# Loading x from ScalarE's queue, shaping the first weight pieces, and letting softmax scalings choose among three engines

## The chip, the cores and the metric

The kernel runs on one core of a Trainium2 chip. The core has five engines that work side by side, each through its own list of instructions in order: PE (TensorE, the matmuls, with a separate track for weight loads), DVE (VectorE), ACT (ScalarE), POOL (GpSimd) and SP (SyncE, which here only issues DMAs). An instruction that waits for a semaphore holds everything behind it on its engine. The metric is the device time of one execution, in microseconds (us), lower being better.

## The reference, cut to what matters

Everything is float32, one batch, 512 positions of width 1024.

```python
# first block: one RG-LRU layer (A), then one sliding-window attention layer (B)
h = rmsnorm(x, norm_g); u = h @ w_in                      # 1024 -> 2*1536
xb, gate = split(u); xb = causal_depthwise_conv(xb, conv_w, conv_b)   # width 4
r = sigmoid(blockdiag(xb, wr) + br); i = sigmoid(blockdiag(xb, wi) + bi)
a = exp(-8 * r * softplus(-lam)); b = sqrt(1 - a*a) * (i * xb)
x = x + (scan(h_t = a_t*h_{t-1} + b_t) * silu(gate)) @ w_out
k, v = rmsnorm(x, kv_g) @ w_kv                            # 2 kv heads of 64, k normed
q, gate = rmsnorm(x, b_norm_g) @ w_in                     # 16 heads of 64, q normed
p = softmax(q k^T * scale + alibi, band of 128, with a sink in the denominator)
x = x + ((p @ v) * silu(gate)) @ w_out
# second block
z = rms_norm(x, norm_mix) @ w_in     # q_a k_a v_a q_b k_b v_b g_a g_b
y_a = windowed_gqa(...)              # 8 heads, 2 kv heads, softmax with a sink
y_b = neighborhood_attn(...)         # 8 heads, 8 x 16 neighbours, a bias table
x = x + (sig(g_a) * (y_a @ w_pa) + sig(g_b) * (y_b @ w_pb)) @ w_out
x = x + relu(rms_norm(x, norm_mlp) @ w_up)**2 @ w_down    # 1024 -> 4096 -> 1024
return rms_norm(x, norm_final)
```

Each attention takes, per head and block of 128 queries, a row of exponentials, their sum, and then the product of the row with 1 / sum. That last product is the "softmax scaling" of the title.

## The kernel before, in words

x is held transposed, as 8 tiles of 128 features by 512 positions. Every large product is made of three matmuls per tile: each operand is split into a high part and a low part (`hi`, `lo`, both in a rounded form of float32), and high times high, high times low and low times high are added up in PSUM. So each weight goes through a DMA (L426) into a raw buffer of the pool `fb`, through an engine that makes the high part (a rounding copy, in the helper A at L307, which may take ACT at L322, POOL at L331 or DVE at L326) and one that makes the low part (a subtraction, TT at L346) into the pool `rb`. The matmuls come from L396, transposes by the identity from L420. The tiles of x are split in the same way, after a multiplication by the norm's weights (ACT L322, then DVE L360). The factor 1 / rms of a position comes later, as a broadcast tile that the outputs are multiplied by.

The order of work is not the program's text. A planner, class `Sched` (L82 to L210), runs while the kernel is built. Every piece of work is a generator (a task) that yields one operation after another; an operation lists the engines that may run it, with an estimated duration for each. At each step the planner picks the task and engine whose operation would end earliest by its model, with a handicap for POOL where there is a choice (AVOID, L36 and L168). What it writes is a fixed list for each engine. The names that the change touches:

- `x_load` (L1692): loads `vec` (all the small vectors) and the 8 tiles of x, each through SP's queue, the later ones held until some weights have been asked for; `x_ready` (L682) starts the split of the tile.
- `raw_task` (L449): issues the weight loads through SP in the order of a list, no more than RAW_MAX ahead; `pieces` (L446) says in what strips a loaded weight is then split; `gemm_pair` (L550) takes the first layer's weights in segments of 4 tiles.
- WARM (L31): ten matmuls on zeros (L1707) at the start. MAXU: how many attention units (a block of queries and a group of heads) may be in flight at once; it limits the tasks of `unit_slot` (L1053).
- `PMUL` (L371, issued at L374): the softmax scaling, which only POOL may run. It is also used for a multiplication of the mask by a column of the queries' deviations (L960).

In an attention unit (`attn_unit`, about L945 to L1040) the order is: scores on PE, a mask and row maximum on DVE (L972), exponentials with their sums on ACT (L322), the reciprocal on DVE (L389), the scaling on POOL (L374), the transposes of the scaled rows on PE (L420), an eviction that splits them (ACT L322, DVE L346), and the product with v on PE. PE takes other tasks' matmuls between these as far as the planner has found any.

DMAs are tracked by eight semaphores, named DMAHW0 to DMAHW7 in the listings below, taken in turn by the loads of all queues. A load that takes a semaphore again waits until that semaphore's previous load has landed.

## Time and profile before

| | |
|---|---|
| time, median of 3 runs | 1137.61 us (1136.96 to 1138.18) |
| profiled execution: its own time | 1139.5 us |
| its span (first to last instruction) | 1137.7 us |
| PE busy | 1119.6 us, 98% of the span |
| DVE, ACT, POOL busy | 758.7, 384.1, 306.6 us (67%, 34%, 27%) |
| mean granted clock of TensorE | 0.994 of full speed |

The profiled execution is 1.9 us (0.17%) above the median; 1.8 us of its time lie outside its span. In the rows, times are us from the start of the span unless they are marked ns. "Idle before" is the time in which the engine had nothing to run, and what ended it stands behind the arrow. A row that stands for several instructions says so with x and their number.

### The profile page before, as it was taken

The page shows a single profiled execution, that of the slowest core. Times are in us where ns is not written, and L with a number is a line of the kernel's source. Part 1 is how long each engine was busy: PE and PEld are TensorE (multiplying, and loading weights), DVE is VectorE, ACT ScalarE, POOL GpSimd, SP SyncE. Part 2 cuts the span into 40 slices and gives each one's busy share as a digit, 9 for nine tenths or more (in the row PEclk, how much of TensorE's full clock was granted, in tenths as well). Part 3 has the DMA queues.
Part 4 walks back from the last instruction along what each step waited for, and adds up shares of the span by engine and source line. Part 5 has one row for each costly group of instructions (what it writes and reads, how often), then busy time and mean ns, then how long its engine had stood idle before and what let it go on. Part 6 is the DMA issues. An engine that isn't in the chain of part 4 may idle for free.

```text
span 1137.7 us, 14747 instructions
## 1 busy us (share of the span) xinstructions
PE 1119.6 (98%) x5316; PEld 931.7 (82%) x5316; DVE 758.7 (67%) x1344; ACT 384.1 (34%) x781; POOL 306.6 (27%) x404
## 2 busy tenths in 40 slices
PE   8999999999999899999999999999999999999997
PEld 6788888888888688788888888888888888888887
DVE  7999998775777886568666565876554225556332
ACT  5457761234566631156444251111111111111001
POOL 1222333135586532032322224312110003113100
PEclk9999999999999899999999999999999999999998
DMA  7333445108133330820463645523233322223001
GB/s 290 87 117 107 145 141 193 56 1 257 40 96 95 134 102 12 238 102 29 134 191 111 176 133 174 185 75 111 79 117 118 112 74 89 78 93 111 1 1 74
DMA packets 46793, 127.42 MB, mean 112 GB/s; under 512 B 6272, under 2 KB 7936, under 8 KB 46720
## 3 DMA queue, kind: packets, MB, share of 16 engines
q1 hardware_dynamic: 46720, 126.47, 35.0%
q8 instruction: 42, 0.69, 0.2%
q14 instruction: 31, 0.25, 0.1%
HBM read 106.53 MB, written 2.10 MB: 95 GB/s over the span
## 4 chain that ended last, share of the span: by engine, by line
PE 93%; DVE 2%; issue 2%; DMA 1%; ACT 1%; POOL 1%; SPq 0%; POOLq 0%; DVEq 0%
PE ps L396 90%; PE ps L420 3%; DVE fb L360 1%; DMA fb<-in_mk 1%; POOL fb L374 0%; DMA fb<-in_x 0%; DVE rb L346 0%; SPq L426 0%; ACT rb L322 0%; DVE fb L346 0%; ACT fb L322 0%; DMA rb<-rb 0%; DVE fb L972 0%; DVE fb L1632 0%; POOLq L1846 0%
## 5 line engine op out<-in xcount | busy, mean ns | idle before, releaser
L396 PE MATMUL ps<-rb 128*128 128x512 f32 (+2 forms) x4856 | 1087.1, 383 | 5.1 <-DMA rb<-rb 1.6
L396 PEld LDWEIGHTS ps<-rb 128*128 128x128 f32 x4856 | 878.0, 188 | 177.6 <-issue 3.0
L331 POOL TENSOR_SCALAR rb<-fb 128x1024 fp32r<-128x1024 f32 (+5 forms) x163 | 175.5, 1087 | 564.2 <-PE ps L396 407.4
L346 DVE TENSOR_TENSOR rb<-fb,rb 128x1024 fp32r<-128x1024 f32 (+5 forms) x305 | 289.0, 972 | 40.9 <-ACT rb L322 37.1
L322 ACT ACTIVATE rb<-fb 128x512 fp32r<-128x512 f32 (+4 forms) x131 | 96.9, 745 | 307.0 <-DVE fb L360 155.4
L346 DVE TENSOR_TENSOR fb<-ps,fb 128x512 f32<-128x512 f32 (+3 forms) x142 | 83.6, 590 | 156.7 <-PE ps L396 141.0
L374 POOL TENSOR_SCALAR fb<-fb,sm 128x256 f32<-128x256 f32 (+2 forms) x128 | 74.9, 603 | 125.3 <-DVE sm L389 97.1
L346 DVE TENSOR_TENSOR fb<-fb 128x512 f32<-128x512 f32 (+1 forms) x120 | 88.9, 747 | 23.3 <-ACT rb L322 21.1
L360 DVE SCALAR_TENSOR_TENSOR fb<-ps,fb 128x512 f32<-128x512 f32 x56 | 38.5, 688 | 58.4 <-PE ps L396 58.3
L346 DVE TENSOR_TENSOR rb<-ps,rb 128x512 fp32r<-128x512 f32 (+2 forms) x86 | 52.3, 612 | 37.5 <-ACT rb L322 35.5
L322 ACT ACTIVATE fb<-fb 128x512 f32<-128x512 f32 (+1 forms) x66 | 39.4, 612 | 102.6 <-DVE fb L346 83.7
L322 ACT ACTIVATE rb<-ps 128x512 fp32r<-128x512 f32 (+2 forms) x86 | 46.0, 538 | 82.1 <-PE ps L420 73.8
L322 ACT ACTIVATE fb<-fb,sm 128x256 f32<-128x256 f32 (+2 forms) x128 | 65.2, 512 | 21.2 <-DVE sm L368 16.1
L322 ACT ACTIVATE rb<-fb,vec 128x512 fp32r<-128x512 f32 x41 | 28.4, 719 | 101.1 <-DVE fb L346 98.9
L322 ACT ACTIVATE fb<-ps 64x256 f32<-64x256 f32 (+2 forms) x68 | 30.1, 442 | 82.5 <-PE ps L396 72.4
L420 PE MATMUL ps<-ident,fb 128*128 128x128 f32 x328 | 52.3, 276 | 5.4 <-POOL fb L374 4.5
L420 PEld LDWEIGHTS ps<-ident,fb 128*128 128x128 f32 x328 | 41.3, 142 | 17.2 <-POOL fb L374 6.2
L972 DVE CUSTOM_DVE_ANT_0 fb<-ps,fb 128x256 f32<-128x256 f32 (+1 forms) x64 | 29.4, 486 | 10.8 <-DMA fb<-in_mk 5.2
L972 DVE CUSTOM_DVE_ANT_0 fb<-ps,fb,sm_qs 128x256 f32<-128x256 f32 (+1 forms) x64 | 27.0, 443 | 7.3 <-PE ps L396 4.9
L374 POOL TENSOR_SCALAR fb<-fb,sm_qt 128x256 f32<-128x256 f32 (+1 forms) x64 | 30.6, 498 | 2.2 <-DMA fb<-in_mk 2.2
L360 DVE SCALAR_TENSOR_TENSOR rb<-fb,vec,rb 128x512 fp32r<-128x512 f32 x41 | 30.5, 763 | 0.6 <-ACT rb L322 0.4
L360 DVE SCALAR_TENSOR_TENSOR fb<-fb,vec 128x512 f32<-128x512 f32 x36 | 30.2, 856 | 0.0
(84 smaller groups left out, 327.0 us busy)
## 6 DMA issues: line engine op xcount, KB each, us to landing
rb<-rb SPq DMA_DIRECT2D x128, 128.0 KB, 2.5
fb<-in_w_down SPq DMA_DIRECT2D x32, 512.0 KB, 3.7
fb<-in_w_in SPq DMA_DIRECT2D x31, 512.0 KB, 4.2
fb<-in_w_up SPq DMA_DIRECT2D x29, 512.0 KB, 3.5
fb<-in_a_w_in SPq DMA_DIRECT2D x22, 512.0 KB, 3.7
fb<-in_b_w_in SPq DMA_DIRECT2D x16, 512.0 KB, 4.7
fb<-in_mb SPq DMA_DIRECT2D x8, 640.0 KB, 5.9
fb<-in_a_w_out SPq DMA_DIRECT2D x8, 512.0 KB, 3.8
```

The lines of the kernel that those rows point to most:

```text
L322: opts = [("ACT", dur, lambda: nc.scalar.activation(out=o, in_=i, func=fn, **kw), TABLES.get(fn))]
L331: lambda: nc.gpsimd.tensor_scalar(out=o, in0=i, scalar1=1.0, scalar2=1.0, op0=ALU.mult, op1=ALU.mult), None,
L346: lambda: nc.vector.tensor_tensor(out=o, in0=a, in1=b, op=op), None,
L360: lambda: nc.vector.scalar_tensor_tensor(out=o, in0=a, scalar=s, in1=b, op0=op0, op1=op1), None,
L374: lambda: nc.gpsimd.tensor_scalar(out=o, in0=a, scalar1=s, scalar2=1.0, op0=ALU.mult, op1=ALU.mult), None,
L396: nc.tensor.matmul(out=o, lhsT=l, rhs=r, start=st, stop=sp)
L420: nc.tensor.transpose(o, i, ident)
L972: nc.vector.tensor_tensor_reduce(out=pt[h], in0=PS[:, b, o0:o0 + nk], in1=m, scale=sc, scalar=-3.0e38, op0=ALU.add, op1=ALU.max, accum_out ...
```

## The change

The 8 loads of x are issued from ScalarE's queue as its first instructions, and the planner is told when each tile lands (3500 + 700 j ns) and that ACT is busy with the issues until 4100 ns. `vec` is still loaded by SP, and the first ten weight loads may follow it at once. The first layer's weights come in segments of 1, 1, 2 and 4 tiles, each split as a whole. x tiles are split with a priority that falls with the tile. WARM goes from 10 to 8, MAXU from 4 to 6. The handicap of POOL becomes a property of the operation, and PMUL may now run on POOL, on ACT (handicap 800 ns) or on DVE (1200 ns).

```diff
-WARM = 10
-MAXU = 4
+WARM = 8
+MAXU = 6
-AVOID = 600.0
@@ Op, Sched.run, A @@
-                        f = s + o[1] + (AVOID if o[0] == "POOL" and len(t.op.opts) > 1 else 0.0)
+                        f = s + o[1] + t.op.late.get(o[0], 0.0)
-        return Op(opts, rd, wr)
+        return Op(opts, rd, wr, {"POOL": 600.0})
@@ PMUL @@
-        return Op([(
-            "POOL", 262.0 + 0.832 * _free(o),
-            lambda: nc.gpsimd.tensor_scalar(
-                out=o, in0=a, scalar1=s, scalar2=1.0, op0=ALU.mult, op1=ALU.mult
-            ), None,
-        )], [a, s], [o])
+        n = _free(o)
+        return Op([
+            ("POOL", 262.0 + 0.832 * n, lambda: nc.gpsimd.tensor_scalar(
+                out=o, in0=a, scalar1=s, scalar2=1.0, op0=ALU.mult, op1=ALU.mult), None),
+            ("ACT", 286.0 + 0.833 * n, lambda: nc.scalar.activation(out=o, in_=a, func=AF.Copy, scale=s), None),
+            ("DVE", 220.0 + 0.524 * n, lambda: nc.vector.tensor_scalar(
+                out=o, in0=a, scalar1=s, scalar2=None, op0=ALU.mult), None),
+        ], [a, s], [o], {"ACT": 800.0, "DVE": 1200.0})
@@ pieces, raw_task, gemm_pair, x_ready @@
-        st = P if i == 0 else 2 * T
-        return [(c, min(c + st, n)) for c in range(0, n, st)]
+        return [(0, n)]
-            yield lambda: i <= pos["s"] or (span(pos["s"], i + 1) <= RAW_MAX and (i < pos["s"] + 2 or fa.room() >= 6))
+            yield lambda: i < 10 or i <= pos["s"] or (span(pos["s"], i + 1) <= RAW_MAX and (i < pos["s"] + 2 or fa.room() >= 6))
-        segs = ksegs(0, kt, 4)
+        segs = [(0, 1), (1, 2), (2, 4), (4, kt)]
-            S.spawn(split_act(x, g, dst, j), -1 if nrm is n_a else 1)
+            S.spawn(split_act(x, g, dst, j), 0.35 * j - 1 if nrm is n_a else 1)
@@ x_load and the start @@
-    def x_load(j):
-        if j == 0:
-            yield DMA(vec, io["vec"])
-        else:
-            yield lambda: pos["r"] > (j + 1) // 2
-        yield DMA(f_(xs[j]), io["x"][j])
-        x_ready(j, [("a_g", act_a)], n_a)
+    def x_load():
+        yield DMA(vec, io["vec"])
+        for j in range(KD):
+            x_ready(j, [("a_g", act_a)], n_a)
         nc.vector.memset(half, -0.5)
+        for j in range(KD):
+            nc.scalar.dma_start(out=f_(xs[j]), in_=io["x"][j])
+            for k in _keys(f_(xs[j])):
+                S.wr[k] = (3500.0 + 700.0 * j, "SP")
+        S.clock["ACT"] = 4100.0
         nc.scalar.activation(out=lt[:, 0, 0:1], in_=eps, func=AF.Exp)
...
-        for j in range(KD):
-            S.spawn(x_load(j), 0.1 * j)
+        S.spawn(x_load(), 0)
```

From `Op` on, lines of the changed kernel are numbered two higher (matmuls L398, transposes L422), later ones a little more. Of the 192 operations that PMUL issues, 153 stand on POOL after the change, 23 on ACT and 16 on DVE.

The first place is ACT's list at the program's start. Before, it begins with the loading of a table of functions and a dummy exponential on `eps`, and then the split of x tile 0 (`rb<-fb,vec`):

```order
L1704 ACT_TABLE_LOAD
L1704 ACTIVATE lt<-eps 128x1 [waits DVE_49]
L322 ACTIVATE rb<-fb,vec 128x512 [waits DMAHW1_49,DMAHW0_49]
L322 ACTIVATE rb<-fb 128x128 [waits DMAHW2_49]
L322 ACTIVATE rb<-fb 128x128 x2
L322 ACTIVATE rb<-fb 128x512 [waits DMAHW3_49]
L322 ACTIVATE rb<-fb,vec 128x512 [waits DMAHW4_49]
L322 ACTIVATE rb<-fb,vec 128x512 [waits DMAHW5_49]
```

After the change the same engine's list begins with the eight loads of x:

```order
L1703 DMA fb<-in_x 128x512 x3
L1703 DMA fb<-in_x 128x512 [waits DMAHW0_49]
L1703 DMA fb<-in_x 128x512 [waits DMAHW3_49]
L1703 DMA fb<-in_x 128x512 [waits DMAHW5_49]
L1703 DMA fb<-in_x 128x512 [waits DMAHW7_49]
L1703 DMA fb<-in_x 128x512 [waits DMAHW1_49]
L1707 ACT_TABLE_LOAD
L1707 ACTIVATE lt<-eps 128x1 [waits DVE_49]
L322 ACTIVATE rb<-fb,vec 128x512 x2
L322 ACTIVATE rb<-fb,vec 128x512 [waits DMAHW6_49]
```

Table load, dummy exponential and the first split now stand behind eight loads, five of which wait for the landing of an earlier load: x3 for x0, x4 for x1, x5 for the second weight of the first group, x6 for the fourth, and x7 (DMAHW1) for a weight load that itself had to wait for `vec`, the semaphore's first user.

The second place is PE's list at the end of layer B's attention, where the last units' scores (128x256), then other matmuls (128x512), then the last transposes (`ident,fb`) and products stand. Before:

```order
L396 MATMUL ps<-rb 128x256 x4
L396 MATMUL ps<-rb 128x512 x3
L420 MATMUL ps<-ident,fb 128x128 x4
L396 MATMUL ps<-rb 128x512 x16
L420 MATMUL ps<-ident,fb 128x128 x4
L396 MATMUL ps<-rb 128x512 x10
L420 MATMUL ps<-ident,fb 128x128 x8
L396 MATMUL ps<-rb 128x512 x3
L420 MATMUL ps<-ident,fb 128x128 x4
L396 MATMUL ps<-rb 128x512 x10
L420 MATMUL ps<-ident,fb 128x128 x4
L396 MATMUL ps<-rb 128x512 x5
```

After, in the same place:

```order
L398 MATMUL ps<-rb 128x256 x8
L398 MATMUL ps<-rb 128x512 x61
L422 MATMUL ps<-ident,fb 128x128 x4
L398 MATMUL ps<-rb 128x512 x15
L422 MATMUL ps<-ident,fb 128x128 x4
L398 MATMUL ps<-rb 128x512 x8
L422 MATMUL ps<-ident,fb 128x128 x4
L398 MATMUL ps<-rb 128x512 x3
L422 MATMUL ps<-ident,fb 128x128 x4
L398 MATMUL ps<-rb 128x512 x10
L422 MATMUL ps<-ident,fb 128x128 x8
L398 MATMUL ps<-rb 128x512 x13
```

All scores are now issued before a run of 61 other matmuls, and all remaining transposes after it; before, the matmuls between the last scores and the run of eight transposes came in smaller runs.

The third place is PE's list at the end of the second block's attention: the last products with v (128x384 and 128x256), then the rest of the projections (128x512). Before:

```order
L420 MATMUL ps<-ident,fb 128x128 x2
L396 MATMUL ps<-rb 128x512 x7
L396 MATMUL ps<-rb 128x384
L396 MATMUL ps<-rb 128x256 x2
L396 MATMUL ps<-rb 128x384 x2
L396 MATMUL ps<-rb 128x256 x2
L396 MATMUL ps<-rb 128x512 x381
```

After:

```order
L422 MATMUL ps<-ident,fb 128x128 x2
L398 MATMUL ps<-rb 128x512 x7
L398 MATMUL ps<-rb 128x384
L398 MATMUL ps<-rb 128x256 x2
L398 MATMUL ps<-rb 128x384 x2
L398 MATMUL ps<-rb 128x256 x2
L398 MATMUL ps<-rb 128x512 x315
```

The run that follows the last product is 66 matmuls shorter: those moved ahead of the attention's end. Counted by the tasks in the planner's order, the first matmul of that run that reads the last attention output (`yb[3]`) is number 79 before and number 13 after.

## Rows read from the trace of the kernel before

**Rows 1.** The page, part 1: busy time, share and instructions of each engine.

```profile
PE 1119.6 (98%) x5316; PEld 931.7 (82%) x5316; DVE 758.7 (67%) x1344; ACT 384.1 (34%) x781; POOL 306.6 (27%) x404
```

**Rows 2.** Waits of PE: releaser, total us, times, longest us.

```profile
PE ps L420 <- POOL fb L374: 4.5, 4, 1.6
PE ps L396 <- DMA rb<-rb: 1.6, 2, 1.4
```

**Rows 3.** Stretches: length, busy time of PE, PEld, DVE, ACT, POOL, granted clock, DMA share, GB/s.

```profile
5.14:15.23 10.09, 8.14 (x31) 5.35 (x29) 8.63 (x17) 8.42 (x16) 0.00 (x0) 1.00 0.98 370
...
389.20:394.60 5.40, 5.40 (x16) 4.33 (x17) 3.73 (x9) 2.39 (x7) 4.72 (x10) 0.50 0.72 245
690.00:1105.00 415.00, 415.00 (x1850) 343.94 (x1849) 220.10 (x278) 55.78 (x76) 73.73 (x73) 1.00 0.30 95
```

**Rows 4.** Timeline of PE, 375 to 396 us: start, us, instruction, idle before.

```profile
379.50 0.60 PE L420 MATMUL ps<-ident,fb 128*128 128x128 f32 x4
379.85 2.57 PE L396 MATMUL ps<-rb 128*128 128x512 f32 x10
384.04 0.33 PE L420 MATMUL ps<-ident,fb 128*128 128x128 f32 x1 [1.62 <-POOL fb L374]
385.51 1.13 PE L420 MATMUL ps<-ident,fb 128*128 128x128 f32 x4 [1.15 <-POOL fb L374]
...
389.05 0.47 PE L420 MATMUL ps<-ident,fb 128*128 128x128 f32 x1 [0.41 <-POOL fb L374]
389.18 1.63 PE L396 MATMUL ps<-rb 128*128 128x512 f32 x3
...
391.31 4.05 PE L396 MATMUL ps<-rb 128*128 128x512 f32 x10
395.20 0.60 PE L420 MATMUL ps<-ident,fb 128*128 128x128 f32 x4
```

**Rows 5.** Timeline of POOL, same stretch.

```profile
382.96 6.04 POOL L374 TENSOR_SCALAR fb<-fb,sm 128x256 f32<-128x256 f32 x8 [6.73 <-DVE sm L389]
```

**Rows 6.** Groups by line and shape: instructions, busy us, mean ns, idle before.

```profile
L374 POOL TENSOR_SCALAR fb<-fb,sm 128x256 f32<-128x256 f32 x80 | 46.1, 589 | 100.3 <-DVE sm L389 94.2 <-issue 3.1 <-ACT rb L322 2.9
L322 ACT ACTIVATE fb<-fb,sm 128x256 f32<-128x256 f32 x80 | 39.7, 498 | 18.2 <-DVE sm L368 16.1 <-DVE sm L360 1.1 <-issue 1.0
L1571 DVE TENSOR_SCALAR fb<-fb,vec 128x256 f32<-128x256 f32 x4 | 1.4, 354 | 0.1
```

**Rows 7.** Timeline of the start, all engines.

```profile
0.72 1.28 ACT L1704 ACT_TABLE_LOAD   x1 [0.72 <-PEq L1839]
0.72 0.38 SPq L426 DMA_DIRECT2D vec<-in_vec  x1
1.17 4.43 PE L1707 MATMUL ps<-warm 128*128 128x512 bf16 x10 [1.17 <-DVE half L1703]
2.01 0.20 ACT L1704 ACTIVATE lt<-eps 128x1 f32<-128x1 f32 x1
4.07 0.72 ACT L322 ACTIVATE rb<-fb,vec 128x512 fp32r<-128x512 f32 x1 [1.86 <-DMA fb<-in_x]
5.14 1.29 PE L396 MATMUL ps<-rb 128*128 128x512 f32 x3
```

**Rows 8.** DMA issues of 0 to 16 us: count, KB each, median us to landing.

```profile
fb<-in_x SPq DMA_DIRECT2D x8, 256.0 KB, 5.6
...
vec<-in_vec SPq DMA_DIRECT2D x1, 93.0 KB, 2.0
```

**Rows 9.** Waits of SP's queue, 0 to 16 us.

```profile
SPq L426 <- DMA fb<-in_x: 2.2, 6, 0.6
```

**Rows 10.** Groups by line and shape that evict the last attention outputs.

```profile
L326 DVE CAST rb<-fb 128x512 fp32r<-128x512 f32 x21 | 9.5, 455 | 0.4
L346 DVE TENSOR_TENSOR fb<-ps,fb 64x512 f32<-64x512 f32 x8 | 5.5, 688 | 1.8 <-ACT fb L322 1.6
L322 ACT ACTIVATE fb<-ps 64x512 f32<-64x512 f32 x8 | 4.7, 593 | 8.4 <-PE ps L396 7.5 <-DVE rb L346 0.9
```

More of the change, by code (lines that the diff above doesn't have):

```diff
@@ L74, with __init__ @@
 class Op:
-    def __init__(self, opts, reads, writes):
+    def __init__(self, opts, reads, writes, late=None):
         self.opts = opts
@@ L82, in __init__ @@
         self.ready = None
+        self.late = late or {}
 class Task:
```

## The prediction

> **What bounds the kernel now.** First the totals of the engines: PE is busy 98% of the span [rows 1], and in a steady stretch it works without a gap, 1850 matmuls in 415.00 us at the full clock, 0.224 us each [rows 3]. The change leaves the matmuls as they are, so only what PE loses against that pace can move: the time before its first real matmul, its waits, and its time at half clock. Next the waits of PE. The reader is to see that they are small, and that one is the largest: transposes that wait for POOL's softmax scalings, 4.5 us in four pieces [rows 2]. Then the timeline around it. A run of ten matmuls starts at 379.85, which at 0.224 ends at 382.09. Eight transposes follow, four of which cost 379.85 − 379.50 = 0.35 us when nothing is late, so 0.70; the next matmul starts at 389.18 [rows 4]. That is 7.09 us for 0.70 of work: 6.4 lost, while POOL works off eight scalings in one run of 6.04 [rows 5]. Behind it the granted clock is 0.50 from 389.20 to 394.60, the lower of its two levels [rows 3]. From 389.18 to 395.20 PE does 13 matmuls and four transposes [rows 4], 2.91 + 0.35 = 3.26 at the pace, in 6.02: 2.8 more. So the stall costs 6.4 + 2.8 = 9.2 us. Last the start: the dummy matmuls run 4.43 us, the first real one starts at 5.14 [rows 7], and up to 15.23 PE does some 29, worth 6.5, in 10.09: 3.6 lost, with the DMA engines 0.98 busy [rows 3].
>
> **The softmax scalings.** The largest term is not the scalings' price but their place. After the change all scores of layer B's last units are issued ahead of 61 other matmuls, 61 × 0.224 = 13.7 us, and only then come the transposes. POOL's eight scalings started 0.87 us after PE's run ended (382.96 against 382.09) and took 6.04 [rows 4, 5]; all that ran in the 7.09 us from the last matmul to the next fits in 13.7. The stall goes, and the low clock behind it, since PE is never idle there. What is late next is the eviction of the transposes and the products, for which the smaller runs between the transposes (15, 8, 3, 10) stand as cover; I leave 0.5 for that: 9.2 − 0.5 = −8.7 us. If the cover were gone, the term would be 0. The engines themselves: 23 scalings on ACT at about the 0.498 of its exponentials of the same shape, 16 on DVE at about 0.354, in place of 0.589 on POOL [rows 6]: 11 us more of ACT, 6 of DVE, 23 less of POOL over the whole run, in engines that are at most 67% busy. I cost them at nothing; PE's matmuls hide them, and in the one place without cover a scaling on DVE ahead of an eviction would cost its 0.354.
>
> **The start.** Here the change adds a wait. ACT's list begins with eight loads, and a load waits for the earlier one on its semaphore; that SP now waits so is seen: six waits for x, up to 0.6 us [rows 9]. On ACT the table load, the dummy exponential and every split stand behind them. The last one, x7, waits for a weight that waits for `vec`. `vec` is issued at 0.72 and lands 2.0 later [rows 7, 8], at 2.7; the weight is issued behind it at 2.9. Its landing takes between 2.0 (`vec`) and 5.6 (a load of x among the others) [rows 8]; I take 3.8, the middle, since it is smaller than x but runs beside seven loads of it. So it lands at 6.7, x7 is issued in some 0.4 (SP takes 0.38 for one), and ACT is free at 7.1 (5.3 to 8.9). Then 1.28 + 0.20 + 0.72 [rows 7]: the first split ends at 9.3, the first matmul is 4.2 later than 5.14 (2.4 to 6.0). Some is taken back: meanwhile nearly all of x and the first weights land, and the 3.6 lost before 15.23 were mostly waits for them. But the splits take ACT 8.42 and DVE 8.63 of those 10.09 us [rows 3], so they cannot be pressed much. I take 2.7 of 3.6 (0 to 3.6). And the clock: eight dummies end at 1.17 + 8 × 0.443 = 4.7, then PE idles 4.6 us. Before, 4.5 us of waiting were followed by 5.4 at half clock [rows 2, 3]; the same here costs up to 2.7, part of which PE would have waited anyway: 2.0 (0 to 2.7). Sum of the start: 4.2 − 2.7 + 2.0 = +3.5, between 2.4 − 3.6 = −1.2 and 6.0 + 2.7 = +8.7. Nothing later takes it up, since the next wait of any size, 1.4 on a copy that moves rows, is the end of the convolution's chain on DVE [rows 2], which begins with the start.
>
> The larger splits, the segments of 1, 1, 2 and 4 tiles, and the loads that SP no longer issues lie within this sum: one split of a whole strip for several, with less fixed time on ACT, but a later first low part.
>
> On one point the Trainium skill speaks against this part. The trace shows the DMA engines 0.98 busy from 5.14 to 15.23 at 370 GB/s, with SP the only issuer [rows 3]. "DMA: Bandwidth & Descriptors", Issuing engines are not separate DMA queues, says that loads of several engines run on the same 16 DMA engines, and that issuing on more of them saves only the time of issuing. By that rule the bytes land no sooner, and nothing of the 3.6 is taken back; by the row alone the 4 us ahead of the first matmul are ones in which the same bytes move. I count it as a rival below.
>
> **The end of the second attention.** MAXU 6 and the cheaper scalings let the planner place 66 matmuls earlier, so that the last attention output now has 12 matmuls of cover, 2.7 us, where it had 78, 17.5 us. Its chain is an eviction on ACT 0.593, a product on DVE 0.688, the high part 0.455 and the low part about as long as the product [rows 10], 2.4 in all. It just fits. With queues ahead of it on DVE it is late by some tenths: +0.5 (0 to 2). MAXU has no other price: units in flight cost buffers, and no wait of PE now is for one.
>
> **Sum.** −8.7 + 3.5 + 0.5 = −4.7. The profiled execution's own time is 1139.5, which becomes 1134.8; it stands 1.9 above the median of the runs, and against that median, 1137.6, the forecast is 1132.9 us. The ends are −9.2 − 1.2 + 0 = −10.4, 1127.2, and −8.7 + 8.7 + 2 = +2.0, 1139.6.
>
> **Rivals.**
> First, slower: the stall moves to the end of the second attention. There the last units' scalings would queue on POOL as at 382.96, and 2.7 us of matmuls are no cover for a run such as the 6.04 [rows 5]. It would cost what it did before, with the low clock: −8.7 + 9.2 + 3.5 = +4.0, 1141.6. It decides when more than about 7 us of scalings, transposes and evictions remain after the last scores there. For it: the run of matmuls behind the last product lost 66. Against it: they were placed ahead, between the last transposes, where they cover the scalings.
>
> Second, the start isn't hurt: the awaited weight lands in 2.0, the loss before 15.23 is taken back in full, and the clock doesn't fall: −1.2 − 8.7 + 0.5 = −9.4, 1128.2. For it: x arrives earlier than now. Against it: a table load, a dummy and a split in series behind all eight issues.
>
> Third, the change doesn't do what it says: 153 of 192 scalings stay on POOL, those of the last units with them, and half of the stall stays as waits for POOL: −4.6 + 3.5 + 0.5 = −0.6, 1137.0. Against it: the 13.7 us of cover don't depend on the engine.
>
> Fourth, nothing is taken back at the start, as the loads land no sooner: 4.2 + 2.0 = 6.2, and −8.7 + 6.2 + 0.5 = −2.0, 1135.6.
>
> **How the numbers follow.** The forecast 0.50, with a range of its own from 1130 to 1136; the first rival 0.15, the second 0.17, the third 0.13, the fourth 0.05. About 0.2%, 2.3 us, is what a measurement of this kernel tells from no change: faster is below 1135.3, slower above 1139.9. Faster: 0.45 of the forecast and the 0.17, 0.62. Same: 0.05 of the forecast, 0.12 of the third, 0.05 of the fourth, 0.22. Slower: the first rival and 0.01, 0.16. The range takes the sum's lower end, and reaches past its upper one until about half of the first rival is in: 1127.5 to 1141.0.
>
> **What would show it.** In the profile after: ACT's table load at about 7 and not at 0.72, the first real matmul at about 9.3, and the granted clock low for a few us behind it; no wait of transposes for POOL near 380, and the clock full there; after the last product of the second attention a gap of less than 1 us. The forecast is wrong if the first matmul starts before 7 or after 11, if transposes wait for a scaling, wherever it runs, for more than 2 us in sum, or if PE waits anywhere after 400 us for more than it does now.

## The result, and the profile after

The changed kernel takes 1146.16 us (median of 6 runs, 1145.32 to 1148.37) against 1137.89 us in the same measurements before: ratio 1.0072, interval 1.0060 to 1.0084. It is slower by 8.3 us, where 4.7 less was forecast, and lies outside the range. Its profiled execution took 1145.7 us, its span 1143.7, 6.0 more than before. The account below is of these two executions, so it has 6.0 to explain and not 8.3: the one before stood above the median of its runs, the one after a little below.

The waits of PE first (releaser, total, times, longest), to be held against [rows 2]:

```profile
PE ps L398 <- ACT rb L322: 8.0, 2, 4.5
PE ps L398 <- DMA rb<-rb: 2.8, 1, 2.8
PE ps L398 <- DVE rb L346: 2.4, 2, 1.9
PE ps L398 <- DVE fb L346: 1.3, 1, 1.3
```

The wait for POOL's scalings is gone, as forecast. In its place stand a wait at the start and one farther on, both for ACT, and the wait for the stacked rows (`rb<-rb`), 1.6 before, is 2.8. Where the time went is seen when all that PE loses against its pace (0.227 us per 512-column matmul, taken from start to start) is added up by place, in us:

| stretch | before | after | difference | what lies there |
|---|---|---|---|---|
| 0 to 100 | 8.1 | 16.5 | +8.4 | first matmul, gate matmuls |
| 100 to 300 | 1.5 | 0.9 | -0.6 | |
| 300 to 350 | 1.4 | 3.1 | +1.7 | a wait for a product on DVE, 1.3 |
| 350 to 400 | 9.9 | 1.3 | -8.6 | the scalings of layer B |
| 400 to 450 | 0.5 | 6.6 | +6.1 | end of layer B's attention |
| 450 to the end | 10.2 | 9.6 | -0.6 | of it +0.8 at 700 to 750, the second attention's end |

The first row counts from the first dummy matmul, and takes the dummies as work; two dummies fewer are 0.4 of its +8.4. The real matmuls are 8.0 late by the end of that stretch, and with 8.0 the column adds up to the 6.0 of the span.

The start, timeline of ACT's queue, ACT and PE, answers to [rows 7]:

```profile
0.72 6.38 ACTq L1703 DMA_DIRECT2D fb<-in_x  x8
7.12 1.28 ACT L1707 ACT_TABLE_LOAD   x1 [7.12 <-DMA fb<-in_x]
8.53 3.77 ACT L322 ACTIVATE rb<-fb,vec 128x512 fp32r<-128x512 f32 x6
9.29 14.94 PE L398 MATMUL ps<-rb 128*128 128x512 f32 x54 [4.52 <-ACT rb L322]
```

The eight issues hold ACT until 7.1, and the first matmul stands at 9.29: both within 0.1 of the forecast. The gate matmuls, which read the stacked outputs of the convolution, stood at 52.81 before. Timeline of PE, and then stretches of the whole core (columns as in [rows 3]):

```profile
54.25 0.73 PE L398 MATMUL ps<-rb 128*128 128x512 f32 x2 [1.94 <-DVE rb L346]
57.78 6.48 PE L398 MATMUL ps<-rb 128*128 128x512 f32 x19 [2.80 <-DMA rb<-rb]
```

```profile
9.27:31.25 21.98, 21.96 (x90) 17.84 (x91) 21.53 (x31) 11.27 (x19) 5.63 (x3) 1.00 0.61 236
31.25:39.04 7.79, 7.79 (x34) 5.83 (x33) 7.38 (x26) 0.60 (x1) 5.34 (x5) 1.00 0.18 63
39.04:57.78 18.74, 14.00 (x62) 10.97 (x60) 18.74 (x31) 7.44 (x11) 1.38 (x1) 0.92 0.21 58
57.78:61.70 3.92, 3.92 (x9) 3.18 (x10) 3.92 (x6) 2.69 (x4) 0.00 (x0) 0.50 0.80 233
```

DVE, the third busy column, has next to no gap from its first split at 9.27 to the gate matmuls: 21.53 of 21.98 us, 7.38 of 7.79, then 18.74 of 18.74. Before, it still had one, and was busy 1.52 of the 4.56 us from 26.14 to 30.70. PE waits twice, 1.94 and 2.80. The granted clock is at its lower level, 0.50, from 54.95, behind the first of the two waits, to 61.77. Now the end of layer B's attention, where [rows 4] showed the old stall; PE, and then the chain of waits from there (start, us, what):

```profile
408.82 3.24 PE L398 MATMUL ps<-rb 128*128 128x512 f32 x13
415.59 0.49 PE L398 MATMUL ps<-rb 128*128 128x512 f32 x1 [3.52 <-ACT rb L322]
416.59 8.70 PE L398 MATMUL ps<-rb 128*128 128x512 f32 x30 [0.51 <-DVE rb L346]
```

```profile
412.10 0.39 ACT fb L322
...
412.52 0.43 DVE fb L346
...
412.97 0.39 ACT fb L322
...
413.38 0.44 DVE fb L346
...
413.84 1.64 DVE fb L346 x2
...
415.50 0.43 DVE rb L326
415.93 0.61 DVE rb L346
...
416.59 3.65 PE ps L398 x8
```

After the last product with v there is nothing left for PE: the run of 13 matmuls that it closes ends at 412.1, and the eviction of that product, the gating and the splits run one after another for 4.45 us. Behind that, 8 matmuls take 3.65 us, the lower clock again. Stall and clock cost 6.1. The other matmuls that could have run there, 33 before, have all been placed earlier: 3 stand inside the run of 13, just ahead of the product's last two, and none behind it.

### The profile page after: what moved, and what is told of

Its sections match the earlier page's. It is cut to its first block, busy times and chain, and to the rows that moved or that the text cites. A ratio compares the mean times of both kernels' runs of the same rounds, so it can differ in the third digit from the quotient of the medians.

```text
span 1143.7 us, 14727 instructions
## 1 busy us (share of the span) xinstructions
PE 1120.2 (98%) x5314; PEld 934.3 (82%) x5314; DVE 772.4 (68%) x1362; ACT 388.5 (34%) x803; POOL 304.8 (27%) x366
## 4 chain that ended last, share of the span: by engine, by line
PE 91%; DVE 5%; issue 2%; DMA 1%; POOL 0%; ACT 0%; SPq 0%; ACTq 0%; DVEq 0%; POOLq 0%
PE ps L398 88%; PE ps L422 3%; DVE fb L346 2%; DVE rb L346 1%; DVE fb L360 1%; DVE rb L360 0%; DVE lt L360 0%; DMA fb<-in_a_w_in 0%; DMA fb<-in_x 0%; DVE fb L973 0%; POOL fb L374 0%; DMA rb<-rb 0%; ACT fb L322 0%; DVE rb L326 0%; SPq L428 0%
## 5 line engine op out<-in xcount | busy, mean ns | idle before, releaser
L398 PE MATMUL ps<-rb 128*128 128x512 f32 (+2 forms) x4856 | 1090.1, 384 | 14.5 <-ACT rb L322 8.0
L398 PEld LDWEIGHTS ps<-rb 128*128 128x128 f32 x4856 | 881.3, 189 | 187.2 <-ACT rb L322 9.4
L331 POOL TENSOR_SCALAR rb<-fb 128x1024 fp32r<-128x1024 f32 (+3 forms) x164 | 197.7, 1216 | 615.3 <-PE ps L398 502.7
L346 DVE TENSOR_TENSOR rb<-fb,rb 128x512 fp32r<-128x512 f32 (+4 forms) x306 | 291.9, 977 | 43.1 <-ACT rb L322 38.7
L322 ACT ACTIVATE rb<-fb 128x512 fp32r<-128x512 f32 (+4 forms) x131 | 92.8, 714 | 298.3 <-DVE fb L360 150.9
L374 POOL TENSOR_SCALAR fb<-fb,sm 128x256 f32<-128x256 f32 (+2 forms) x105 | 57.8, 567 | 111.5 <-DVE sm L391 70.9
L422 PE MATMUL ps<-ident,fb 128*128 128x128 f32 x328 | 50.9, 273 | 1.0 <-DVE fb L1572 0.9
L422 PEld LDWEIGHTS ps<-ident,fb 128*128 128x128 f32 x328 | 41.0, 141 | 11.3 <-DVE fb L1572 1.1
L360 DVE SCALAR_TENSOR_TENSOR rb<-fb,vec,rb 128x512 fp32r<-128x512 f32 x41 | 33.0, 820 | 2.6 <-ACT rb L322 2.5
L360 DVE SCALAR_TENSOR_TENSOR fb<-fb 128x512 f32<-128x512 f32 x32 | 29.1, 917 | 0.0
L360 DVE SCALAR_TENSOR_TENSOR fb<-fb,vec 128x512 f32<-128x512 f32 x36 | 27.6, 797 | 0.0
```

Source lines behind the costliest of these rows:

```text
L322: opts = [("ACT", dur, lambda: nc.scalar.activation(out=o, in_=i, func=fn, **kw), TABLES.get(fn))]
L331: lambda: nc.gpsimd.tensor_scalar(out=o, in0=i, scalar1=1.0, scalar2=1.0, op0=ALU.mult, op1=ALU.mult), None,
L346: lambda: nc.vector.tensor_tensor(out=o, in0=a, in1=b, op=op), None,
L360: lambda: nc.vector.scalar_tensor_tensor(out=o, in0=a, scalar=s, in1=b, op0=op0, op1=op1), None,
L374: ("POOL", 262.0 + 0.832 * n, lambda: nc.gpsimd.tensor_scalar(out=o, in0=a, scalar1=s, scalar2=1.0, op0=ALU.mult, op1=ALU.mult), None),
L398: nc.tensor.matmul(out=o, lhsT=l, rhs=r, start=st, stop=sp)
```

## The experiments

Times are medians, the ratio is to the kernel before on the same chip. Two tables serve all of them. The first gives the starts, in us, of the 1st, 79th and 251st real matmul, worked out from the records of each trace; the 251st lies behind the gate matmuls and the lower clock there.

```
kernel       1st    79th   251st        kernel       1st    79th   251st
before       5.14   25.57  67.45        segs_only    4.87   26.47  74.24
after        9.29   29.50  75.43        segs_lam     5.06   26.07  67.23
warm20       9.34   29.32  75.70        lamafter     9.34   29.60  74.44
tablefirst  12.09   32.75  78.03        after_lam    9.74   30.17  74.85
xsplit       4.79   29.98  75.72        xinter_lam   4.80   28.98  74.01
xinter       5.11   28.85  75.80        queue_only  11.29   33.87  73.67
```

| kernel | us | ratio, 95% interval | kernel | us | ratio, 95% interval |
|---|---|---|---|---|---|
| start_only | 1154.21 | 1.0145, 1.0131-1.0159 | queue_only | 1151.42 | 1.0125, 1.0109-1.0140 |
| pmul_maxu | 1137.37 | 0.9991, 0.9982-1.0000 | segs_only | 1142.09 | 1.0043, 1.0030-1.0057 |
| warm20 | 1146.21 | 1.0074, 1.0060-1.0088 | hold_two | 1131.94 | 0.9954, 0.9942-0.9967 |
| tablefirst | 1148.49 | 1.0099, 1.0083-1.0115 | after_lam | 1145.34 | 1.0061, 1.0049-1.0074 |
| xsplit | 1145.94 | 1.0076, 1.0064-1.0088 | segs_lam | 1143.92 | 1.0052, 1.0040-1.0065 |
| lamafter | 1147.79 | 1.0089, 1.0076-1.0102 | after_both | 1145.62 | 1.0068, 1.0051-1.0085 |
| pmul_only | 1139.89 | 1.0016, 1.0008-1.0025 | maxu_only | 1147.74 | 1.0091, 1.0077-1.0105 |
| hold_last | 1134.85 | 0.9977, 0.9968-0.9987 | xinter_lam | 1143.66 | 1.0058, 1.0045-1.0072 |
| xinter | 1147.17 | 1.0088, 1.0074-1.0102 | | | |

**The two halves.** `start_only`, the changed kernel without its other half:

```diff
-MAXU = 6
+MAXU = 4
-("ACT", 286.0 + 0.833 * n, ...), ("DVE", 220.0 + 0.524 * n, ...)
```

> The changed kernel with MAXU back at 4 and the scalings back on POOL alone: what is left is the start (x from ScalarE's queue, 8 dummies, weight segments 1, 1, 2, 4). Theory S (the start costs more than its late first matmul, through the chain on DVE that ends in the gate matmuls at 52.8 before and 57.8 after): first matmul at 9.3, a wait of 3 to 5 us near 52 to 58 with the lower clock behind it, 8 us lost more than before by 62 us, so about 1146. Rival E (the start costs only the 3.0 us that are lost more by 50 us, the rest is the end of layer B's attention): about 1141.

`pmul_maxu`, the kernel before with MAXU 6 and the three options of PMUL:

```diff
-MAXU = 4
+MAXU = 6
+("ACT", 286.0 + 0.833 * n, ...), ("DVE", 220.0 + 0.524 * n, ...)
```

> The kernel before with only MAXU 6 and the scalings on three engines: the start is that of before. Theory E (the matmuls placed ahead of the last transposes of layer B's attention are missing behind its last product with v): the transposes no longer wait for POOL (-9), but PE waits 3 to 5 us for the eviction of the last output, with the lower clock behind it (+6): about 1135. If that wait doesn't appear here: 1129. If this part is what made the change slower: 1143 or more.

`start_only` lost 17.4 us by 100 us, as the changed kernel does (16.5), and then had both stalls in layer B, the scalings' 3.7 and the eviction's; hence 1154. (Both figures count from the first dummy, as in the table above.) `pmul_maxu` has no wait for the scalings, and the eviction's in its place:

```profile
401.34 2.28 PE L399 MATMUL ps<-rb 128*128 128x512 f32 x8
407.61 0.79 PE L399 MATMUL ps<-rb 128*128 128x512 f32 x1 [3.99 <-ACT rb L323]
```

So theory E held, and the loss is the start's; this half alone is worth about nothing (1137.37, against some 1135 expected).

**The matmuls of layer B's end.** The filler there are the first six k-steps of four output tiles of `b_w_out`: 24 steps of three, 72 matmuls. In the kernel before, 39 of them stood ahead of the last product with v and 33 behind it; in the changed kernel all 72 stand ahead, among the transposes and in front of them. `hold_last` adds to `pmul_maxu` that the last of the four tiles waits until the attention's last transposes are written; `hold_two` that the last two wait:

```diff
+        if cfg.get("last"):                      # unit (3, 3) of the sliding window
+            flags.add("s_last")
         ob = yield from pa.get()
@@ gemm_open @@
+                    if lo == 0 and n == 3 and w == "b_w_out":     # hold_two: n == 2
+                        yield lambda: "s_last" in flags
```

> As the kernel with MAXU 6 and the scalings on three engines and the start of before (1137.4), but the last 18 of the 72 matmuls are held back until the attention's last transposes are written. Theory E: they stand behind the last product and cover 4 us of the 4.3 + low clock that PE waited for its eviction, so -5 to -7: about 1131. If they are missed at the scalings instead: a wait for transposes of several us there, and 1136 to 1138.

> As the kernel in which 18 matmuls were held back until the attention's last transposes, with 36 held: 8 us of matmuls behind layer B's last product, 69 ahead of its last transposes. Theory E: no wait for the last eviction is left, nor the lower clock behind it, 3 to 4 us less: about 1131. If 69 are too few for the scalings: waits of the transposes come back, 1135 to 1138.

In `hold_last`, with 15 matmuls behind the last product, the wait at the eviction was 1.53 + 0.91 in place of 3.99 + 0.21, and the time 1134.85 where about 1131 was expected. In `hold_two`, with 30, PE runs through behind the last transposes; ahead of them it has four short waits, the longest 0.37 for a scaling. Its timeline, and below it its waits:

```profile
393.52 1.42 PE L423 MATMUL ps<-ident,fb 128*128 128x128 f32 x11 [0.37 <-POOL fb L375]
394.70 25.61 PE L399 MATMUL ps<-rb 128*128 128x512 f32 x111
```

```profile
PE ps L399 <- ACT rb L323: 1.7, 2, 1.5
PE ps L399 <- DMA rb<-rb: 1.6, 2, 1.4
...
PE ps L423 <- POOL fb L375: 0.4, 1, 0.4
```

111 matmuls behind the last transposes take 25.61 us, 0.23 each, at the full clock. At 1131.94 us `hold_two` beats both kernels, by 5.5 us the kernel before. Theory E is shown.

**Three engines or six units.** Each of the two edits alone, on the kernel before (`pmul_only`, `maxu_only`; the lines are those of `pmul_maxu`):

> The kernel before with only the scalings on three engines, MAXU 4. Behind layer B's last product some 29 matmuls stand ahead of the first that needs its output (33 before, none with MAXU 6). Theory E (72 matmuls in all can be placed there, and both the scalings and the last eviction live on them): no wait for the eviction, and the wait for the scalings is shortened by 13 more matmuls ahead of the last run of transposes and by the other engines' help: 1129 to 1132. If the scalings still wait as before: 1138.

> The kernel before with only MAXU 6: all scalings on POOL. With six units in flight 57 matmuls stand ahead of the last run of layer B's transposes (before: runs of 3 to 16), and some 11 between its last product and the first that needs its output. If it was the six units, not the three engines, that took away the wait for the scalings: no wait of transposes of more than 1 us in sum near 390, and a wait of 2 to 3 for the last eviction with the lower clock behind it. Then the second attention's end, with 303 matmuls in its last run like the kernels that waited 2 us there: 1137 to 1141 in all. If POOL alone is too slow even so: 3 to 4.5 us of waits for L374 stay, 1142 or more.

`pmul_only` missed: POOL again ran eight scalings in one go, and the transposes waited for it as before (the second timeline is POOL's):

```profile
388.22 0.69 PE L423 MATMUL ps<-ident,fb 128*128 128x128 f32 x2 [2.33 <-POOL fb L375]
```

```profile
383.49 6.08 POOL L375 TENSOR_SCALAR fb<-fb,sm 128x128 f32<-128x128 f32 x8 [6.79 <-ACT sm L323]
```

In `maxu_only` no transpose waited for POOL at all: it was the six units that removed that wait. Its time, 1147.74 where 1137 to 1141 was expected, is bad for other places: 2.4 and 1.6 at the eviction, and waits of 2 us near 333 and 711, each with the lower clock behind it. So the three engines are not idle in this change: beside six units they are worth some 10 us (1137.37 against 1147.74), at 300 to 350 and 700 to 750 and not at the wait that they were meant for.

**The clock at the start.** `warm20`:

```diff
-WARM = 8
+WARM = 20
```

> The changed kernel with 20 dummy matmuls in place of 8, every list else the same: PE is busy almost until its first real matmul, which stays at 9.3. If the lower clock from 9.3 to 14.0 costs its full price, 4.7 us at half speed are 2.3 lost: about 1144. If the splits on ACT and DVE set the pace there and the clock costs nothing: 1146.

The first two rows are the changed kernel's, the other two those of `warm20`:

```profile
9.34:14.00 4.66, 4.66 (x10) 3.41 (x11) 4.66 (x11) 4.13 (x7) 0.00 (x0) 1.00 1.02 388
14.00:29.00 15.00, 15.00 (x67) 12.38 (x66) 14.55 (x19) 7.08 (x13) 5.63 (x3) 1.00 0.56 220
```

```profile
9.34:14.00 4.66, 4.38 (x12) 3.27 (x13) 4.66 (x11) 4.02 (x7) 0.00 (x0) 0.69 1.02 389
14.00:29.00 15.00, 15.00 (x66) 12.40 (x66) 14.55 (x19) 7.23 (x13) 5.56 (x3) 0.98 0.57 225
```

The 1.00 of the very first row is no measurement, for that trace has no entry of the clock before 13.98: ten matmuls in 4.66 us, 0.47 each, against 67 in 15.00, 0.22 each, show the lower level. In `warm20` the full level came in part of that stretch, 0.69 in the mean, with 12 matmuls in place of 10, and nothing came of it: the 79th matmul came 0.18 earlier and the 251st 0.27 later. `warm20` alone doesn't show what a full clock all through would give. The traces bound it: the 15th matmul waits for DVE's split of a tile of x, which ends at 14.69, and at 14.74 in `warm20`, and the matmul starts at 14.97 and 14.81. So the clock could give back some 0.2 or 0.3 us there. Up to that matmul the splits pace PE; from 14 to 29 us PE has work ahead of it and runs at its own pace.

**ACT's queue and the loads.** `tablefirst` puts the table load and the dummy exponential ahead of the loads; `xsplit` leaves x0 to x2 on ACT and lets SP load the rest behind four weights, `xinter` between the weights:

```diff
+            if j < 3:
                 nc.scalar.dma_start(out=f_(xs[j]), in_=io["x"][j])
@@ raw_task, xinter: {3: (3,), 5: (4, 5), 7: (6, 7)} @@
+            if i == 3:
+                for j in range(3, KD):
+                    nc.sync.dma_start(out=f_(xs[j]), in_=io["x"][j])
```

> The changed kernel with the table load and the dummy exponential issued ahead of the eight loads of x on ScalarE's queue, every list else the same. If ACT's list in order is what holds the first split (table load 1.28 and exponential 0.20 behind the last issue at 7.1), the first matmul comes at 8 to 8.5 in place of 9.3 and the time falls by about 1, to 1145. If the loads, now issued 1.5 later, are what the splits wait for: first matmul at 9.3 or later, 1146 to 1147.

> The changed kernel with only x0 to x2 loaded from ScalarE's queue (none of them waits) and x3 to x7 from SP's, behind the first four weight pieces; all other lists the same. Theory H (ACT held by its eight issues): ACT is free at 2.1, the first matmul comes at 4.8 to 5.2 in place of 9.3, and the gate matmuls that stood at 57.8 come 3 to 5 us earlier: 1141 to 1143. Rival L (the last tiles of x and the weights land no sooner, and the chain hangs on them): the first matmul comes early, but PE waits again before 16, and the gate matmuls move by less than 1: 1145.5.

> The changed kernel with x0 to x2 from ScalarE's queue and x3 to x7 from SP's, put between the weights (x3 behind four pieces, x4 and x5 behind six, x6 and x7 behind eight); all other lists the same. Theory V (DVE's list runs without a gap from its first split of x to the gate matmuls, so what counts is when both the x tiles and the weights in its first rows have landed): the second pair of weights, which DVE waited for until 11.4 with x3 to x7 ahead of it, lands at about 8, DVE starts its run some 3 us sooner than at 9.3, and the gate matmuls come at 54 to 55 in place of 57.8: 1141 to 1143. Rival L (the bytes of x and weights together set the pace whatever the order): gate matmuls at 57 to 58, 1145 to 1146.

`tablefirst` went the other way: the loads waited longer for each other, the last issue ended at 11.3 and the first matmul came at 12.09. In `xsplit` and `xinter` ACT was free, the first matmul came at 4.8 and 5.1, and no time was won by the 251st. DVE's list waits there for weights that now lie behind x; the row is from the timeline of DVE in `xsplit`:

```profile
11.43 0.62 DVE L326 CAST rb<-fb 128x256 fp32r<-128x256 f32 x2 [2.56 <-DMA fb<-in_a_w_in]
```

My theory that the held queue is the cause fell, at least while something else held DVE's list too.

**The chain of the decay parameter.** It consists of 17 operations of 12 elements on DVE (`lt`, `cneg`), started when 7 weight units are taken: `yield lambda: pos["u"] > 6`. In the changed kernel it stands in one piece ahead of the convolution's first evictions:

```profile
32.55 1.32 DVE L346 TENSOR_TENSOR fb<-ident,col_a 128x512 f32<-128x512 f32 x1
33.79 3.72 DVE L360 SCALAR_TENSOR_TENSOR lt<-lt 128x12 f32<-128x12 f32 x6
37.42 0.17 DVE L368 TENSOR_SCALAR lt<-vec 128x12 f32<-128x12 f32 x1
```

`lamafter` held it until the third stacked output; then each half of the start was tried alone on the kernel before: `queue_only` (x from ACT's queue) and `segs_only` (strips, segments, first ten loads, priorities). `after_lam` and `segs_lam` put the condition at 12 units:

```diff
-        yield lambda: pos["u"] > 6
+        yield lambda: pos["u"] > 6 and ("stk", 2) in flags     # lamafter
+        yield lambda: pos["u"] > 11                            # after_lam, segs_lam
```

> The changed kernel with the chain of 12-element operations on the decay parameter (lt, cneg, on DVE) not started before the third output of the convolution is stacked. Theory D (those operations, 33.8 to 38.2 on DVE ahead of the first eviction behind the norm's broadcast, hold the convolution's chain by 3.4 us): the first eviction comes at about 35.8 in place of 39.0 and the gate matmuls at about 54.4 in place of 57.8. Rival: the chain is limited elsewhere, gate matmuls at 57 or later. Farther on the planner writes another order, with some 31 matmuls between layer B's last product and the first that needs its output (3 in the changed kernel): by theory E no wait there, -6 more. Time by D and E with no scaling wait 1137, by neither 1146.

> The kernel before with only the loads of x moved to ScalarE's queue (and the planner told so); strips, segments, dummies, MAXU and scalings as before. Theory V: ACT is held to about 7, DVE has next to nothing to do until 9, and the gate matmuls come 4 to 6 us later than at 52.8, with the lower clock behind the longer wait: 1143 to 1146. Rival (the strips and segments are what costs): gate matmuls near 53, 1138 to 1139.

> The kernel before with only the weights' strips and segments of 1, 1, 2, 4, the first ten loads at once, and the falling priority of x splits; x from SP's queue in the places of before. Theory V: the first splits start with x0 as before, gate matmuls at 52 to 54, and with layer B's stall for the scalings left in: 1137 to 1140. Rival (strips and segments cost): 1143 or more.

> The kernel before with only the strips, segments, first ten loads and priorities, and the same condition (12 units). By theory W the 250th matmul, at 74.2 with the segments alone and 67.5 before, comes at 68 to 70; by the rival at 73 to 74. The end of layer B's attention is written in another order here (149 matmuls in its last run, like the changed kernel's 148), so that by theory E a wait for the last eviction with its lower clock, some 6, comes in: time 1139 to 1143 by W.

> The changed kernel with one condition different: the decay parameter's 12-element chain starts when 12 weight units are taken, not 7 (the segments of 1, 1, 2, 4 make twice as many units of the first outputs, so that 7 are taken much sooner than before). On DVE it is again spread among the convolution's operations, its exponential on ACT still ahead of the change of table; the end of layer B's attention is written as in the changed kernel. Theory W (the segments moved the chain by that count, and its run on DVE ahead of the first evictions holds the gate matmuls): first eviction at about 36, gate matmuls at 54 to 55.5 in place of 57.8, a shorter wait: 1140 to 1143. Rival (the chain's place is worth under 1 us; late weights and x are all): 1145 to 1146.

`segs_only` alone cost 6.8 us by the 251st matmul, against what I expected, though its first matmul was early. `segs_lam` gave all of it back: 67.23 against 67.45 before. So the segments cost nothing by themselves up to there; they make 8 units of the first pair of outputs where there were 4, and a count of units started the chain too soon. The first rows are PE's timeline at the gate in `segs_only`, then that in `segs_lam`:

```profile
50.93 0.73 PE L396 MATMUL ps<-rb 128*128 128x512 f32 x2 [1.39 <-DVE rb L346]
54.55 1.85 PE L396 MATMUL ps<-rb 128*128 128x512 f32 x5 [2.89 <-DMA rb<-rb]
```

```profile
50.95 1.42 PE L396 MATMUL ps<-rb 128*128 128x512 f32 x5 [1.07 <-DMA rb<-rb]
```

(Its total of 1143.92 is no better, since the planner wrote layer B's end in the order with the eviction's wait, 3.8 us and the lower clock.) `queue_only` cost 6.2 there, its first matmul at 11.29; the rest of its time, above the 1143 to 1146 expected, is lost farther on, in waits of 3.1 at 148, 3.0 for scalings and 2.1 at 717. In the changed kernel the two overlap: with the chain mended (`after_lam`) the gate matmuls came 2.6 earlier, at 55.17, but PE still waited 1.90 and 1.04, the clock fell as before, and the 251st gained 0.6; the time, 1145.34, missed the 1140 to 1143 expected. `lamafter` gained 1.0 there, with two more table loads on ACT around its late exponential. Layer B's eviction wait was gone in it, but the transposes waited 2.0 for scalings and PE 2.8 at 485.8, and 1147.79 missed the expectation by far.

Last, `xinter_lam` takes away the held queue and the early chain, `after_both` the early chain and layer B's wait (by the held matmuls of `hold_two`):

> As the changed kernel with the decay chain started at 12 units (250th matmul at 74.9), with x3 to x7 loaded by SP between the weights, so that ACT isn't held and the first matmul comes at 5.1. If the chain on DVE had hidden the gain of the earlier loads: gate matmuls at 53 to 54 in place of 55.2, no lower clock there, 250th matmul at 68 to 71. If the first rows of DVE's list wait for weights that now lie behind x (theory L): gate matmuls at 55, 250th matmul at 74 or more.

> The changed kernel with both mended: the condition at 12 units, and 36 of the 72 matmuls held back until layer B's last transposes are written. By W and E together 3 to 5 and 6 less than 1146.2: 1135 to 1137, that is level with the kernel before, the rest being the late first matmul. If either fails: 1140 or more.

`xinter_lam` sides with theory L: the gate at 54.5, the 251st matmul at 74.01. Against `after_lam` the held queue is worth 0.8 us there; what remains is that DVE's list, written for x landing early, waits for weights. `after_both` has no wait at layer B's end, and loses 2.1 from 400 to 450 where `after_lam` loses 7.9; but it has a new wait at the end of the second attention, with the lower clock behind it, 6.0 in all, and so came to 1145.62 where 1135 to 1137 was expected:

```profile
707.83 1.76 PE L398 MATMUL ps<-rb 128*128 128x512 f32 x8 [0.15 <-POOL rb L331]
711.52 10.86 PE L398 MATMUL ps<-rb 128*128 128x512 f32 x33 [1.92 <-DVE rb L326]
```

That is the place that the prediction's first rival named, but not its mechanism, for no scaling was waited for. It is the chain of the section on the second attention's end, an eviction on ACT (0.60, from 709.63), a product on DVE (0.70) and a cast (0.49), which had found its cover in the changed kernel and found none here.

## Why the prediction was wrong

**The scalings: right in place and size.** 9.2 forecast for the stall and its clock, 8.6 measured. The reason given held, 61 matmuls stand ahead of the transposes. It did not say which half brings them: the six units in flight do, and the three engines do nothing for this wait (`maxu_only` has none of it, `pmul_only` waits 5.0 for POOL).

**The step that failed.** "What is late next is the eviction of the transposes and the products, for which the smaller runs between the transposes (15, 8, 3, 10) stand as cover; I leave 0.5". It measured 6.1. The smaller runs lie ahead of the last product with v; behind it no other matmul was left, where there had been 33: 3.52 and 0.51 of waiting, and the lower clock behind them. The stock of 72 was moved forward whole: 24 of it are among the 61 (33 others of these belong to `b_w_in`, the attention's own input weights, and 4 are products with v), the other 48 stand between the transposes. The forecast counted the cover where it had come, and not where it had gone from; `hold_two` shows that 36 held back pay for both. I made this very count for the second attention's end (12 left of 78, +0.5 forecast, +0.8 measured) and not here. Of the 10.7 us between the forecast of -4.7 and the +6.0 of the span, this step makes 5.6 and the start, below, 4.5. The third of the prediction's signs of being wrong, a longer wait of PE after 400 us, is what came.

**The start.** ACT free at 7.1 and first matmul at 9.3 came out as forecast, but by luck. `vec` landed at 3.76 and not at 2.7, and the weight behind it, issued at 3.77, took 2.6 and not 3.8; it had landed before x7's turn. What held ACT was x5's wait for a weight that landed at 5.77, and three issues of 0.34 to 0.44 behind it. Of the sum of +3.5 two terms were wrong and cancelled, by luck too. The clock, +2.0, was worth some 0.2 or 0.3 at most (the section on `warm20`). And -2.7 taken back was 0.2: 4.15 late at the first matmul, 3.93 late at the 79th. That is the number of the fourth rival, which takes nothing back, but not its reason, that the loads land no sooner. They did: x's third tile at 5.59 in place of 8.35, the last at 12.12 in place of 14.13, as more was moved from 4 to 9 us (before, then after):

```profile
4.00:9.00 5.00, 3.93 (x11) 1.63 (x9) 3.55 (x9) 3.26 (x7) 0.00 (x0) 1.00 0.83 286
4.00:9.00 5.00, 0.77 (x2) 0.00 (x0) 1.99 (x8) 1.86 (x3) 0.00 (x0) 1.00 1.06 375
```

From 8.53 on ACT split six tiles of x in 3.77 us without waiting for one; what held PE was the splits themselves, on ACT and DVE, which began 4 us late. Once the DMA engines were busy, two issuers moved no more than one: 1.02 of the time and 388 GB/s from 9.34 to 14.00, against 0.98 and 370 [rows 3]. The rule of the Trainium skill ("DMA: Bandwidth & Descriptors", Issuing engines are not separate DMA queues), that issuing on more engines saves only the time of issuing, agrees with the rows of the busy stretches.

**"Nothing later takes it up"** failed on the other side. The delay grew from 3.9 to 8.0 between the 79th and the 251st matmul. I had read the end of the convolution's chain as a wait of 1.4 on a DMA [rows 2], and not that DVE would have next to no gap in all that stretch. So a later start moves the gate, and what the list holds ahead of it counts; PE's cover there ends, and the waits bring the lower clock, which the wait of before did not. The chain of the decay parameter, moved by a count of weight units, was in the diff's consequences and in none of my terms; alone it was worth 7.0 (`segs_only` against `segs_lam`). In the changed kernel mending it gave only 0.6 of the 4.1 by which the delay grew (`after_lam`).

**Not foreseen** either: 1.7 at 300 to 350, where layer B's first units stand in another order; no run tests that this order is the cause. What stays open is how much of the start is left when both lists and loads are ordered for each other: with x from SP between the weights and the chain mended 6.6 remain at the 251st matmul, and no run split these between the order of DVE's list and the order of the loads.

## What to carry to other kernels

Matmuls that cover a wait are a stock: when a scheduler puts more of them ahead of one wait, count how many are left behind the next, and hold some back on purpose. Where an engine off the critical path has next to no gaps between the start and a point that PE waits for, a delay or a small operation ahead of that point can reach PE. And a condition that counts pieces (weight units here) changes its meaning when a change cuts the pieces smaller.

## What the runs showed of the hardware

Six operations of 12 elements in a row on DVE took 3.72 us (in `segs_only` 3.43), three of them about 1 us each and three 0.18, while POOL ran rounding copies of 128x768 from 32.50 to 36.88; from the chain of the work that ended last there:

```profile
33.87 0.93 DVE lt L360
...
35.83 1.07 DVE lt L360
36.93 0.18 DVE lt L360
```

"SBUF — State Buffer", SBUF: two separate sides, of the Trainium skill says that VectorE and GpSimd share a pair of ports under an exclusive lock, and that an instruction of VectorE with two inputs in SBUF, as these have, and a GpSimd instruction that reads SBUF block each other for the whole instruction. These rows agree, but no run took POOL's work away to show it.

The lower clock came at the gate behind a wait of 1.94 (after) and not behind the 1.38 of before or the 1.07 of `segs_lam`. At the start it cost some 0.2 or 0.3 us at most, behind the gate more: 9 matmuls in 3.92 us from 57.78 to 61.70, about 1.9 lost.

Eight loads issued from ACT's queue, five of them with a wait, held ACT for 6.38 us, and for 8.37 in `queue_only`, where the weights that they shared semaphores with came later.
